# Samples' queries and one mixing step moved among the value tiles, softmax steps of the samples set one to two pages apart, two sizes of a split table changed

## The chip, the cores and the metric

One Trainium2 chip, one of its cores. The time is that of one execution on the device, in microseconds (us). The kernel before takes 904.75 us (median of 3 runs, 904.45 to 905.07). Engines are named as in the profile: PE (matrix products), PEld (its weight loads), DVE (vector), ACT (scalar functions), POOL (general) and SP (issues most DMAs).

## The reference

One layer of a decoder for 512 prompt rows and 8 sample rows (one new token each, 4096 cached positions in 32 pages of 128). Cut to what the change touches:

```python
z = rmsnorm(x) @ w_in
u, v = gelu(z[OFF_U:OFF_V]), gelu(z[OFF_V:])          # 512 columns each
q = rope(rmsnorm(...))                                # 8 heads, 64 + 32
sg = u * (einsum('gts,bcsgd->bctgd', tril(w_s), v) + b_s)   # mixing in chunks of 128 rows
# a sample b attends to its 4096 cached rows c and itself:
k_n = rmsnorm(einsum('bkr,rhd->bkhd', c, w_uk)) * k_norm_w
p = softmax((q_nope @ k_n + q_rope @ k_rope) * SCALE)
attn = (p @ c) @ w_uv
h = x + concat(attn, sg) @ w_o
h = h + conv_ffn(rmsnorm(h)); ...
```

## The kernel before

A product in full float32 precision is made of three products of a high and a low part (`mm3`, L148 to L151), so nearly all PE work carries the lines L149, L150 and L151. `split` (L135) makes the parts: ACT casts the high one (L138 or L140), DVE or POOL subtracts (L133, L146). The scheduler of the tile framework sets the order on each engine from the program's order, the readiness that it estimates and the hints `issue_after` (not before that instruction) and `keep_in_program_order`; engines work through their order strictly, and the same order runs every time.

**Value tiles.** The rows are five tiles: 0 to 3 of 128 prompt rows, 4 of the 8 samples. `v_mm(t)` makes v of a tile with 24 products of 128x512 and ACT takes its gelu out of PSUM (`v_out`, L520). `mix(t)` then multiplies v, split into `sq` tiles, with the masked table `wsr`, whose mask is applied on DVE (L883) and which is split into `wsh` (ACT) and `wsl` (DVE, L133). The program's order is `v_mm(4)`, the table, `v_mm(0)`, `mix(4)`, `v_mm(1)`, `mix(0)`, `v_mm(2)`, `mix(1)`, `v_mm(3)`, then the load of the function table with exp and ln (`preload_act_table_set`, L898), `mix(2)`, `mix(3)`; the prompt's first head is transposed in between (`t_step`, L645).

**Samples' queries.** In front of all that stand, for the 8 samples: eight transposes of the queries (L484), their scaling into `qgT` (L485), the score of the own key `snall` (L486 to L494), the product of queries and `w_ukT` (L500) into `qtil` (L502), and `qbd`, the rotary part (L506).

**Pages.** `s_page` handles one cached page of one sample: six products (`mm3` twice) into one of three PSUM tiles `mm`, ACT squares them (L761) and copies out the scores (`raw`, L762), DVE sums the squares (`ss`, L763) out of one of three `sq` tiles. A page's PSUM tile is free when `raw` has been copied. There are 32 pages to a sample and 256 in all: two in each of the prompt's 16 attention blocks, the rest, for samples 1 to 7, one behind the other. The softmax of sample b is spread over the pages of sample b+1 by a table of steps, page number to work (`steps`, L812 ff.): variance and ln, exp and square, the factor on `raw`, the correction (`newton`), the addition to the scores, maxima, their transpose (L794), `mx_all` (L797, L798), their broadcast by PE (`mx_b`, L801), subtraction, exp, sum, and the product with the values (L838). For the last sample it runs beside the first products with `w_o` (`o_half`). SGS names the groups of four pages behind which a part of the mixed rows `sgr` is split for those products.

Of the kernel before, what the change touches and what calls it, by code (L numbers as in the profile page):

```python
# [39 lines left out]
NG = 10  # L40
NAT = 8
KRQ = 4
SGS = (51, 54, 59, 62)
EF = 3
PF = 2

# [2 lines left out]
def trunk_step(ctx: ExitStack, tc: tile.TileContext, I, O):  # L49
# [429 lines left out]

    qs_, ks_ = qtok[4], ktok[4]  # L480
    qgT = const([96, 8, 8], F32, "qgT")
    ps = ms()
    for h in range(8):
        nc.tensor.transpose(ps[:96, h * 8:h * 8 + 8], qs_[:8, h * DQ:(h + 1) * DQ], ident[:8, :8])  # L484
    nc.vector.tensor_scalar(qgT.rearrange("p h b -> p (h b)"), ps[:96, 0:64], gq96[:, 0:1], None, op0=ALU.mult)  # L485
    nc.vector.tensor_mul(h96(ks_, 8)[:, :, 0:DN], h96(ks_, 8)[:, :, 0:DN], gqk8[:, 0:1].to_broadcast([8, 8, DN]))  # L486
    nc.vector.tensor_mul(qs_[:8, 0:768], qs_[:8, 0:768], ks_[:8, 0:768])
    snew = S()
    nc.vector.tensor_reduce(snew[:8, 0:8], h96(qs_, 8), axis=AX.X, op=ALU.add)
    nc.vector.tensor_scalar(snew[:8, 0:8], snew[:8, 0:8], SCALE, None, op0=ALU.mult)  # L490
    snall = const([128, 8, 8], F32, "snall")
    nc.gpsimd.memset(snall, NEG)
    nc.vector.tensor_mul(snall[:8], eye8[:, 0].rearrange("p (b h) -> p b h", b=8), snew[:8, 0:8].unsqueeze(1).to_broadcast([8, 8, 8]))
    nc.vector.tensor_add(snall[:8], snall[:8], eye8[:, 1].rearrange("p (b h) -> p b h", b=8))  # L494

    wukT = WR()
    nc.sync.dma_start(wukT[0:64, 0:1024], I["w_ukT"])
    ps = ms()
    for h in range(8):
        nc.tensor.matmul(ps[:, h * 8:h * 8 + 8], wukT[0:64, h * 128:(h + 1) * 128], qgT[0:64, h], start=True, stop=True)  # L500
    qtil = const([128, 8, 8], F32, "qtil")
    nc.vector.tensor_copy(qtil.rearrange("p h b -> p (h b)"), ps[:, 0:64])  # L502
    qbd = const([128, 8, 4, 8], F32, "qbd")
    nc.gpsimd.memset(qbd, 0.0)
    for j in range(4):
        nc.scalar.copy(qbd[32 * j:32 * j + 32, :, j, :], qgT[64:96].rearrange("p h b -> p b h"))  # L506


    bsb = G()
# [12 lines left out]
    def v_mm(t):  # L522
        t0, n = TOK[t]
        sl = slice(t0, t0 + n)
        ps = mm()[:n, 0]
        for j in range(4):
            wh, wl = wget(k_v[j], 3 - j)
            for i in range(2):
                mm3(ps, xh[j][:, i, sl], xl[j][:, i, sl], u3(wh, 2, 512)[:, i], u3(wl, 2, 512)[:, i],
                    j == 0 and i == 0, j == 3 and i == 1)  # L530
        v_out(t, ps)

    def mix(t):
        t0, n = TOK[t]
        v = vg[t]
        if t == 3:
            nc.sync.dma_start(O["vp"], v[:, 0:512])
        if t == 4:
            nc.sync.dma_start(O["vs"], v[:8, 0:512])
            mx = G()  # L540
            m3 = mx[:8, 0:512].rearrange("p (g d) -> p g d", g=8)
            nc.vector.tensor_mul(m3, v[:8, 0:512].rearrange("p (g d) -> p g d", g=8), ws8[:, 0].unsqueeze(2).to_broadcast([8, 8, 64]))
            nc.vector.tensor_add(m3, m3, ws8[:, 1].unsqueeze(2).to_broadcast([8, 8, 64]))
            ps = ms()
            for gp in range(4):
                nc.tensor.transpose(ps[:, gp * 8:gp * 8 + 8], mx[:8, gp * 128:(gp + 1) * 128], ident[:8, :8])
# [75 lines left out]

    pq_ = {}

    def prep_items(hp):

        qk = [None] * 4
        pq_[hp] = [None, qk]
# [11 lines left out]
        def t_step(c, w):  # L640
            h = 2 * hp + c
            src, sc = ((qtok, gq96), (ktok, None))[w]
            ps = ms()
            for t in range(4):
                nc.tensor.transpose(ps[:96, t * 128:(t + 1) * 128], src[t][:, h * DQ:(h + 1) * DQ], ident)  # L645
# [124 lines left out]
    def s_softmax(b):  # L770
# [24 lines left out]

        def mx_all():
            nc.vector.tensor_reduce(m2[:8, 0:1], hold["t"][:8, 0:128], axis=AX.X, op=ALU.max)  # L797
            nc.vector.tensor_scalar(m2[:8, 8:16], ident[:8, 0:8], m2[:8, 0:1], None, op0=ALU.mult)  # L798

        def mx_b():  # L800
            after_keys(lambda: nc.tensor.matmul(hold["t"][:, 128:136], ones[:8], m2[:8, 8:16], start=True, stop=True))  # L801
# [2 lines left out]
            nc.gpsimd.tensor_scalar(ss, ss, 1.0 / DN, EPS, op0=ALU.mult, op1=ALU.add)  # L804
            act(y0, ss, AF.Ln)

        def rstd():
            act(y0, y0, AF.Exp, scale=-0.5)
            act(t, y0, AF.Square)

        with_qbd[16] = mx_t
        steps.update({  # L812
            4: var,
            5: rstd,
            6: lambda: nc.vector.tensor_mul(raw, raw, y0),
            7: lambda: newton(raw, ss, raw, t),
            8: lambda: nc.vector.tensor_add(sc[:, 0:256], sc[:, 0:256], raw),
            9: lambda: nc.vector.tensor_reduce(m1[:, 0:8], s3.rearrange("p c h -> p h c"), axis=AX.X, op=ALU.max),
            17: mx_all,
            20: mx_b,  # L820
            21: lambda: nc.vector.tensor_sub(s3, s3, hold["t"][:, 128:136].unsqueeze(1).to_broadcast([128, 33, 8])),
            23: lambda: act(sc, sc, AF.Exp),
            24: lambda: nc.vector.tensor_reduce(psum[:, 0:8], s3.rearrange("p c h -> p h c"), axis=AX.X, op=ALU.add),
            27: lambda: s_pv(b),
            29: lambda: s_out(b),
        })
# [81 lines left out]
    blocks = [(hp, qb) for hp in range(4) for qb in range(4)]  # L908
    pa_score(0, 0)
# [360 lines left out]
```

## Time and profile before

| what | value |
|---|---|
| median of 3 runs | 904.75 us |
| the profiled execution's own time | 907.9 us |
| its span, first to last instruction | 906.0 us |
| granted PE clock, mean | 0.989 of full |
| DVE, ACT, POOL busy | 645.2, 503.6, 215.0 us (71%, 56%, 24%) |
| table loads on ACT (ACT_TABLE_LOAD) | 9, of 1.28 us each |
| value tiles 0 to 3 | from 81.9 to 117.4 us |
| pages of samples 1 to 7 alone | from about 204 to 408 us |

Busy time of an engine is the time in which one of its instructions runs; a product on PE overlaps the next one. The granted clock is the share of full speed that PE was given in a stretch.

### The profile page before, as it was taken

The page shows a single profiled execution, that of the slowest core. Times are in us where ns is not written, and L with a number is a line of the kernel's source. Part 1 is how long each engine was busy: PE and PEld are TensorE (multiplying, and loading weights), DVE is VectorE, ACT ScalarE, POOL GpSimd, SP SyncE. Part 2 cuts the span into 40 slices and gives each one's busy share as a digit, 9 for nine tenths or more (in the row PEclk, how much of TensorE's full clock was granted, in tenths as well). Part 3 has the DMA queues.
Part 4 walks back from the last instruction along what each step waited for, and adds up shares of the span by engine and source line. Part 5 has one row for each costly group of instructions (what it writes and reads, how often), then busy time and mean ns, then how long its engine had stood idle before and what let it go on. Part 6 is the DMA issues. An engine that isn't in the chain of part 4 may idle for free.

```text
span 906.0 us, 20621 instructions
## 1 busy us (share of the span) xinstructions
PE 884.8 (98%) x7847; PEld 843.4 (93%) x7847; DVE 645.2 (71%) x1093; ACT 503.6 (56%) x1182; POOL 215.0 (24%) x243
## 2 busy tenths in 40 slices
PE   8998999999999999999999999999999999999997
PEld 6896878889999999889999999999999999999997
DVE  6579676668888898796669776337775437766774
ACT  6573368778888888784446443124443224455561
POOL 4004851237777777730000000000000000000000
PEclk9999999999999999999999999999999999999999
DMA  6332160243667664613332222322222322323311
GB/s 220 99 97 82 48 186 1 80 137 98 180 186 214 190 194 135 203 59 110 84 122 88 89 88 75 113 94 94 94 93 71 116 94 83 97 84 100 117 59 60
DMA packets 65347, 100.43 MB, mean 111 GB/s; under 512 B 13841, under 2 KB 47770, under 8 KB 65250
## 3 DMA queue, kind: packets, MB, share of 16 engines
q1 hardware_dynamic: 63202, 94.93, 33.2%
q0 software_dynamic: 2048, 4.20, 1.8%
q8 instruction: 62, 1.02, 0.5%
q14 instruction: 35, 0.29, 0.1%
HBM read 95.95 MB, written 3.15 MB: 109 GB/s over the span
## 4 chain that ended last, share of the span: by engine, by line
PE 77%; DVE 7%; ACT 6%; issue 4%; DMA 3%; SPq 3%; POOL 1%; ACTq 0%; POOLq 0%; DVEq 0%
PE mm L149 23%; PE mm L150 23%; PE mm L151 23%; DVE ss L763 2%; SPq L605 2%; PE ms L838 1%; ACT sq L761 1%; ACT wr L670 1%; PE ms L697 1%; PE ms L149 1%; DMA wr<-w_u 1%; PE ms L151 1%; PE ms L150 1%; DVE wr L673 1%; PE ms L156 1%
## 5 line engine op out<-in xcount | busy, mean ns | idle before, releaser
L149 PE MATMUL mm<-u,w 128*128 128x260 f32 x1392 | 395.2, 284 | 0.1
L151 PE MATMUL mm<-u,w 128*128 128x260 f32 x1392 | 394.7, 284 | 0.0
L150 PE MATMUL mm<-u,w 128*128 128x260 f32 x1392 | 394.1, 283 | 0.0
L150 PEld LDWEIGHTS mm<-u,w 128*128 128x128 f32 x1392 | 263.0, 189 | 0.2
L151 PEld LDWEIGHTS mm<-u,w 128*128 128x128 f32 x1392 | 262.8, 189 | 0.2 <-issue 0.2
L149 PEld LDWEIGHTS mm<-u,w 128*128 128x128 f32 x1392 | 262.5, 189 | 0.5 <-PE mm L151 0.2
L133 DVE TENSOR_TENSOR w<-wr,w 128x1024 fp32r<-128x1024 f32 (+1 forms) x94 | 112.6, 1199 | 106.1 <-issue 54.0
L763 DVE TENSOR_REDUCE ss<-sq 128x8 f32<-128x512 f32 x256 | 166.8, 678 | 26.4 <-ACT sq L761 21.9
L138 ACT CAST w<-wr 128x1024 fp32r<-128x1024 f32 (+1 forms) x94 | 96.5, 1031 | 140.4 <-PE mm L151 127.1
L761 ACT ACTIVATE sq<-mm 128x512 f32<-128x512 f32 x256 | 153.1, 610 | 33.2 <-PE mm L151 18.7
L149 PE MATMUL mm<-wuk,a 128*128 128x260 f32 x416 | 123.4, 297 | 2.5 <-ACT raw L762 2.1
L151 PE MATMUL mm<-wuk,a 128*128 128x260 f32 x416 | 118.4, 285 | 0.0
L150 PE MATMUL mm<-wuk,a 128*128 128x260 f32 x416 | 118.3, 284 | 0.0
L149 PEld LDWEIGHTS mm<-wuk,a 128*128 128x128 f32 x416 | 79.1, 190 | 8.2 <-ACT raw L762 6.3
L150 PEld LDWEIGHTS mm<-wuk,a 128*128 128x128 f32 x416 | 79.1, 190 | 0.0
L151 PEld LDWEIGHTS mm<-wuk,a 128*128 128x128 f32 x416 | 79.0, 190 | 0.0
L592 POOL DMA_INDIRECT wr<-krT,idx x64 | 62.4, 974 | 14.1 <-issue 6.4
L1082 ACT ACTIVATE a<-abuf,cst 128x512 f32<-128x512 f32 x44 | 35.9, 816 | 39.9 <-DVE abuf L1080 38.8
L1083 DVE SCALAR_TENSOR_TENSOR a<-abuf,cst,a 128x512 f32<-128x512 f32 x44 | 33.0, 751 | 25.7 <-ACT a L1082 25.4
L133 POOL TENSOR_TENSOR a<-u,a 128x512 fp32r<-128x512 f32 x34 | 44.2, 1301 | 17.0 <-ACT a L719 15.0
L762 ACT COPY raw<-mm 128x8 f32<-128x8 f32 x256 | 44.5, 174 | 0.0
L138 ACT CAST u<-a 128x520 fp32r<-128x520 f32 x24 | 15.1, 627 | 43.7 <-DVE a L1121 43.3
(307 smaller groups left out, 1324.4 us busy)
## 6 DMA issues: line engine op xcount, KB each, us to landing
wr<-w_ffi SPq DMA_DIRECT2D x44, 512.0 KB
u<-pages SPq DMA_DIRECT2D x152, 128.0 KB
w<-pages SPq DMA_DIRECT2D x104, 128.0 KB
wr<-w_ffo SPq DMA_DIRECT2D x16, 512.0 KB
wr<-w_o SPq DMA_DIRECT2D x8, 512.0 KB
wr<-w_pg SPq DMA_DIRECT2D x8, 512.0 KB
wr<-w_ffo SPq DMA_DIRECT2D x8, 384.0 KB
a<-xT SPq DMA_DIRECT2D x8, 260.0 KB
```

Of the source, the lines that this page charges most:

```text
L133: return (nc.vector if eng == "v" else nc.gpsimd).tensor_sub(dl, src, dh.bitcast(F32))
L138: nc.scalar.copy(dh, src)
L149: nc.tensor.matmul(out, lh, rh, start=start, stop=False)
L150: nc.tensor.matmul(out, lh, rl, start=False, stop=False)
L151: return nc.tensor.matmul(out, ll, rh, start=False, stop=stop)
L592: nc.gpsimd.indirect_dma_start(krT[:, g * 128:(g + 1) * 128], None, I["krT"], bass.IndirectOffsetOnAxis(ap=idx.bitcast(U32)[:, b * 8 + g:b ...
L605: page_dma.append(nc.sync.dma_start(pv[:, j], I["pages"][bass.ds(rs[j], 1)].rearrange("a p f -> (a p) f")))
L761: squares.append(nc.scalar.activation(u3(sq, 2, 256), ps[:, :, 0:256], AF.Square))
L762: nc.scalar.copy(raw[:, c * 8:c * 8 + 8].rearrange("p (a h) -> p a h", a=2), ps[:, :, 256:260])
L763: nc.vector.tensor_reduce(ss[:, c * 8:c * 8 + 8], sq.rearrange("p (h d) -> p h d", d=DN), axis=AX.X, op=ALU.add)
L1082: nc.scalar.activation(c[:, 0:T], a[:, 2:T + 2], AF.Identity, scale=cw[:, m, 2:3], bias=cw[:, m, 3:4])
L1083: nc.vector.scalar_tensor_tensor(c[:, 0:T], a[:, 1:T + 1], cw[:, m, 1:2], c[:, 0:T], op0=ALU.mult, op1=ALU.add)
```

## The change

Four edits:

1. The samples' queries become `s_queries(after)` (transposes, `qgT`, `qbd`, `snall`), called behind `v_mm(1)` with its last product as `after`; the product with `w_ukT` becomes `s_folded`, behind `v_mm(2)`. `mix(4)` moves behind `v_mm(1)`. The memsets of `snall` and `qbd` stay in front.
2. `mix(2)` moves in front of the load of the function table. The first head's transposes all come behind `v_mm(3)`.
3. Softmax steps: 4, 5, 6, 7, 8, 9 become 3, 4, 5, 6, 7, 9, 10, 12: exp and square are two steps, `newton` is two steps. `mx_all` 17 to 18, `mx_b` 20 to 21, subtraction 21 to 22, exp 23 to 24, sum 24 to 25. In `mx_all` the product of the unit matrix and the maximum is a `tensor_mul` with a broadcast operand in place of a `tensor_scalar`.
4. SGS becomes (59, 60, 62, 63) from (51, 54, 59, 62).

```diff
-SGS = (51, 54, 59, 62)
+SGS = (59, 60, 62, 63)
...
-    ps = ms()
-    for h in range(8):
-        nc.tensor.transpose(ps[:96, h * 8:h * 8 + 8], qs_[:8, h * DQ:(h + 1) * DQ], ident[:8, :8])
-    nc.vector.tensor_scalar(qgT.rearrange("p h b -> p (h b)"), ps[:96, 0:64], gq96[:, 0:1], None, op0=ALU.mult)
...
+    def s_queries(after):
+
+        ps = ms()
+        with tc.issue_after(after.ins):
+            for h in range(8):
+                nc.tensor.transpose(ps[:96, h * 8:h * 8 + 8], qs_[:8, h * DQ:(h + 1) * DQ], ident[:8, :8])
+        nc.vector.tensor_scalar(qgT.rearrange("p h b -> p (h b)"), ps[:96, 0:64], gq96[:, 0:1], None, op0=ALU.mult)
...
+    def s_folded(after):
+        ps = ms()
+        with tc.issue_after(after.ins):
+            for h in range(8):
+                nc.tensor.matmul(ps[:, h * 8:h * 8 + 8], wukT[0:64, h * 128:(h + 1) * 128], qgT[0:64, h], start=True, stop=True)
+        nc.vector.tensor_copy(qtil.rearrange("p h b -> p (h b)"), ps[:, 0:64])
...
-            nc.vector.tensor_scalar(m2[:8, 8:16], ident[:8, 0:8], m2[:8, 0:1], None, op0=ALU.mult)
+            nc.vector.tensor_mul(m2[:8, 8:16], ident[:8, 0:8], m2[:8, 0:1].to_broadcast([8, 8]))
...
-            4: var,
-            5: rstd,
+            3: var,
+            4: lambda: act(y0, y0, AF.Exp, scale=-0.5),
+            5: lambda: act(t, y0, AF.Square),
             6: lambda: nc.vector.tensor_mul(raw, raw, y0),
-            7: lambda: newton(raw, ss, raw, t),
...
     v_mm(0)
-    mix(4)
-    p0 = prep_items(0)
-    p0 = prep_items(0)
-    v_mm(1)
+    v1 = v_mm(1)
+    s_queries(v1)
+    mix(4, v1)
     mix(0)
-    p0[0]()
-    v_mm(2)
+    v2 = v_mm(2)
+    s_folded(v2)
     mix(1)
-    p0[1]()
-    p0[2]()
-    v_mm(3)
+    v3 = v_mm(3)
+    mix(2)
     tc.keep_in_program_order(nc.scalar.preload_act_table_set("natural_log_exp_and_others"))
     wuv = G()
...
-    mix(2)
+    p0 = prep_items(0, v3)
+    for f in p0[:4]:
+        f()
     mix(3)
-    p0[3]()
     p0[4]()
```

Behind line 480 the changed kernel's line numbers are higher by 7 to 12: L898 is L906 there, the gelu L520 is L527, the softmax's functions L781 are L793, the exp of the prompt L670 is L682.

The order on ACT behind value tile 2, before (the rows end with the prompt's first exp, L670; `g` is a gelu's result or the high part of a head, `sq` the high part of a value tile, `a` and `g` from `ms` the first head's parts):

```order
L520 ACTIVATE g_1306<-mm_1281,rtok 128x512
L898 ACT_TABLE_LOAD
L138 CAST sq_1467<-g_1306 128x512
L138 CAST a_1498<-ms_1493 96x512
L637 COPY g_1507<-ms_1502 128x512
L670 ACTIVATE wr_1521,s_1519<-mm_1509,s_1518 128x128 x2
```

and of the change:

```order
L138 CAST sq_1281<-g_1216 128x512
L906 ACT_TABLE_LOAD
L527 ACT_TABLE_LOAD
L527 ACTIVATE g_1279<-mm_1254,rtok 128x512
L140 ACTIVATE g_1444<-ms_1439,gq_385 96x512
L138 CAST sq_1476<-g_1279 128x512
L138 CAST g_1453<-ms_1448 96x512
L140 ACTIVATE a_1462<-ms_1457,gq_385 96x512
L138 CAST a_1471<-ms_1466 96x512
L646 COPY g_1507<-ms_1502 128x512
L682 ACT_TABLE_LOAD
L682 ACTIVATE wr_1521,s_1519<-mm_1509,s_1518 128x128 x2
```

The load that the program asks for now stands ahead of value tile 3's gelu; a load for the gelu stands behind it, and one for exp ahead of the prompt's first exp. In all there are 29 table loads on ACT, 9 before: these two more, two at each of the eight softmaxes, and two at the norm ahead of the feed-forward part.

The order on ACT in the softmax of sample 0, among the pages of sample 1 (L761 and L773 the square of a page, L762 and L774 its scores), before:

```order
L762 COPY raw_2634<-mm_2718 128x8
L781 ACTIVATE g_2613<-ss_1553 128x256
L761 ACTIVATE sq_2738<-mm_2731 128x512
L762 COPY raw_2634<-mm_2731 128x8
L781 ACTIVATE g_2613<-g_2613 128x256
L761 ACTIVATE sq_2751<-mm_2744 128x512
```

and of the change:

```order
L774 COPY raw_2634<-mm_2689 128x8
L793 ACT_TABLE_LOAD
L793 ACTIVATE g_2613<-ss_1553 128x256
L773 ACTIVATE sq_2727<-mm_2720 128x512
L774 COPY raw_2634<-mm_2720 128x8
L793 ACT_TABLE_LOAD
L793 ACTIVATE g_2613<-g_2613 128x256
L773 ACTIVATE sq_2739<-mm_2732 128x512
```

A table load now stands ahead of the ln and another, one page later, ahead of the exp; before there was none at either.

The order on DVE behind the key tiles of the prompt, which makes the table for `mix(0)` (`w` the masked table, `wr` its low part, `u` and `g` queries and keys), of the change:

```order
L473 TENSOR_TENSOR u_653<-u_653,g_577 128x8x32
L893 TENSOR_TENSOR w_1070<-w_1070,cst 128x1024
L373 TENSOR_TENSOR g_857<-u_653,g_573 128x256
L374 TENSOR_TENSOR g_857<-u_653,g_573 128x8x16
L375 TENSOR_TENSOR g_857<-u_653,g_573 128x8x16
L499 TENSOR_TENSOR u_580<-u_580,cst 8x8x64
L376 TENSOR_TENSOR u_653<-g_857 128x8x32
L133 TENSOR_TENSOR wr_1074<-w_1070,wr_1073 128x1024
L133 TENSOR_TENSOR sq_1166<-g_1102,sq_1165 128x512
```

Before, L485 stood where L893 stands, and L883 and the split of `wr` came nine and fifteen rows behind it. On PE the eight transposes L495 now stand behind all 48 products of value tiles 0 and 1, and directly behind them the products of `mix(0)`; before they stood (as L484) among the products of value tile 0, and those of `mix(0)` behind tile 1 and beside tile 2.

More of the change, by code (lines that the diff above doesn't have):

```diff
@@ L481, in trunk_step @@
     qgT = const([96, 8, 8], F32, "qgT")
-    ps = ms()
-    for h in range(8):
-        nc.tensor.transpose(ps[:96, h * 8:h * 8 + 8], qs_[:8, h * DQ:(h + 1) * DQ], ident[:8, :8])
-    nc.vector.tensor_scalar(qgT.rearrange("p h b -> p (h b)"), ps[:96, 0:64], gq96[:, 0:1], None, op0=ALU.mult)
[L486 to L489, printed above, removed]
@@ L490, in trunk_step @@
-    nc.vector.tensor_scalar(snew[:8, 0:8], snew[:8, 0:8], SCALE, None, op0=ALU.mult)
     snall = const([128, 8, 8], F32, "snall")
+    qtil = const([128, 8, 8], F32, "qtil")
+    qbd = const([128, 8, 4, 8], F32, "qbd")
     nc.gpsimd.memset(snall, NEG)
-    nc.vector.tensor_mul(snall[:8], eye8[:, 0].rearrange("p (b h) -> p b h", b=8), snew[:8, 0:8].unsqueeze(1).to_broadcast([8, 8, 8]))
-    nc.vector.tensor_add(snall[:8], snall[:8], eye8[:, 1].rearrange("p (b h) -> p b h", b=8))
+    nc.gpsimd.memset(qbd, 0.0)
@@ L528, in v_mm, with mix @@
             for i in range(2):
-                mm3(ps, xh[j][:, i, sl], xl[j][:, i, sl], u3(wh, 2, 512)[:, i], u3(wl, 2, 512)[:, i],
-                    j == 0 and i == 0, j == 3 and i == 1)
+                last = mm3(ps, xh[j][:, i, sl], xl[j][:, i, sl], u3(wh, 2, 512)[:, i], u3(wl, 2, 512)[:, i],
+                           j == 0 and i == 0, j == 3 and i == 1)
         v_out(t, ps)
-    def mix(t):
+        return last
+    def mix(t, after=None):
         t0, n = TOK[t]
@@ L545, in mix @@
             for gp in range(4):
-                nc.tensor.transpose(ps[:, gp * 8:gp * 8 + 8], mx[:8, gp * 128:(gp + 1) * 128], ident[:8, :8])
+                with tc.issue_after(after.ins):
+                    nc.tensor.transpose(ps[:, gp * 8:gp * 8 + 8], mx[:8, gp * 128:(gp + 1) * 128], ident[:8, :8])
             for gp in range(4):
@@ L623, in trunk_step, with prep_items @@
     pq_ = {}
-    def prep_items(hp):
+    def prep_items(hp, after=None):
         qk = [None] * 4
@@ L643, in t_step @@
             ps = ms()
-            for t in range(4):
-                nc.tensor.transpose(ps[:96, t * 128:(t + 1) * 128], src[t][:, h * DQ:(h + 1) * DQ], ident)
+            with ExitStack() as es:
+                if after:
+                    es.enter_context(tc.issue_after(after.ins))
+                for t in range(4):
+                    nc.tensor.transpose(ps[:96, t * 128:(t + 1) * 128], src[t][:, h * DQ:(h + 1) * DQ], ident)
             th, tl = (A(F32R), A(F32R)) if c else (G(F32R), G(F32R))
```

38 lines of the change are left out of this document (19 added, 19 removed).

## The prediction

> **What bounds the kernel now.** I read the page first, then PE's waits, then the granted clock in stretches.
>
> ```profile
> span 906.0 us, 20621 instructions
> PE 884.8 (98%) x7847; PEld 843.4 (93%) x7847; DVE 645.2 (71%) x1093; ACT 503.6 (56%) x1182; POOL 215.0 (24%) x243
> PE mm L149 <- ACT raw L762: 2.9, 10, 0.8
> PE ms L484 <- DVE u L376: 2.6, 1, 2.6
> PE ms L801 <- DVE s L798: 1.9, 1, 1.9
> ```
>
> PE is busy for 884.8 of 906.0 us, so it is the bound, and only 21.2 us of idle time can be won without giving it less work. The change takes no product away. The three waits are those that it aims at: 2.9 us in ten pieces for PSUM tiles of the pages, 2.6 us once for the samples' queries, 1.9 us once for the maxima. Whatever makes PE wait anew is paid in full, and it may be paid twice, as the clock shows in stretches of 3.41 us (the first number is the stretch's length, the second PE's busy time; the third last column is the granted clock):
>
> ```profile
> 84.00:87.41 3.41, 1.15 (x11) 1.04 (x12) 3.41 (x10) 0.00 (x0) 3.41 (x2) 1.00 0.00 0
> 87.41:90.83 3.42, 3.42 (x10) 2.64 (x9) 3.42 (x9) 1.38 (x5) 3.42 (x2) 0.50 0.00 0
> 90.83:94.24 3.41, 3.41 (x23) 2.86 (x23) 3.41 (x5) 0.52 (x1) 3.41 (x5) 1.00 0.03 5
> 94.24:97.65 3.41, 3.41 (x10) 2.66 (x9) 3.41 (x6) 2.36 (x5) 3.41 (x3) 0.50 0.00 0
> 118.13:121.54 3.41, 2.42 (x20) 2.06 (x19) 2.62 (x7) 2.53 (x4) 3.33 (x5) 1.00 0.84 248
> 121.54:124.96 3.42, 3.42 (x47) 3.27 (x49) 2.17 (x6) 0.59 (x1) 1.37 (x5) 1.00 0.80 221
> 363.90:367.32 3.42, 1.56 (x14) 1.33 (x12) 3.42 (x4) 2.22 (x8) 3.24 (x4) 1.00 0.21 58
> 367.32:370.73 3.41, 3.41 (x16) 3.41 (x16) 2.43 (x5) 1.06 (x3) 0.72 (x1) 0.50 0.65 186
> ```
>
> On this grid the clock is 1.00 or 0.50 for a whole stretch. A stretch with 2.26 us idle (84.00) or 1.86 us (363.90) is followed by one at half clock, which costs 3.41 / 2 = 1.7 us; one with 0.99 us idle (118.13) is not. The stretch from 90.83 is full, but more than half of it are the small products L500, and it too is followed by half clock. So idle time above some point between 0.99 and 1.86 us in a stretch costs 1.7 us more.
>
> **The table loads.** The order of the change has 29 loads of ACT's function table, the order before 9. The end of the kernel before shows what ln and exp cost where the common table is not loaded:
>
> ```profile
> 859.76 1.28 ACT L165 ACT_TABLE_LOAD   x1
> 861.05 0.64 ACT L165 ACTIVATE g<-g 128x520 f32<-128x520 f32 x1
> 861.71 1.28 ACT L166 ACT_TABLE_LOAD   x1
> 863.00 0.64 ACT L166 ACTIVATE g<-g 128x520 f32<-128x520 f32 x1
> ```
>
> One load takes 861.05 - 859.76 = 1.29 us of ACT's time, and ln followed by exp needs two. In the change the load that the program asks for runs ahead of value tile 3's gelu, which loads another table; so every softmax of a sample now has two loads, one page apart. The Trainium skill (ScalarE: Activation LUTs, What ACT_TABLE_LOAD costs) has the same 1283 ns, but adds a drain of about 1380 ns to each switch. The rows show no drain: the function behind the load starts 0.01 us after it; by that page each load would cost twice as much.
>
> **Pages.** Seven of the softmaxes run among pages that stand one behind the other. How much ACT can be late there, before:
>
> ```profile
> 348.20 0.28 PE L149 MATMUL mm<-wuk,a 128*128 128x260 f32 x1
> 352.55 0.28 PE L149 MATMUL mm<-wuk,a 128*128 128x260 f32 x1
> 349.12 0.60 ACT L761 ACTIVATE sq<-mm 128x512 f32<-128x512 f32 x1
> 349.62 0.16 ACT L762 COPY raw<-mm 128x8 f32<-128x8 f32 x1
> 352.41 0.62 ACT L761 ACTIVATE sq<-mm 128x512 f32<-128x512 f32 x1
> 352.94 0.47 ACT L781 ACTIVATE g<-g 128x256 f32<-128x256 f32 x1
> 353.25 0.64 ACT L761 ACTIVATE sq<-mm 128x512 f32<-128x512 f32 x1
> 353.73 0.46 ACT L781 ACTIVATE g<-g 128x256 f32<-128x256 f32 x1
> 354.04 0.21 ACT L762 COPY raw<-mm 128x8 f32<-128x8 f32 x1
> 354.31 0.39 PE L149 MATMUL mm<-wuk,a 128*128 128x260 f32 x1 [0.16 <-ACT raw L762]
> ```
>
> The first two rows are the first products of pages six apart: 0.725 us a page. A page begun at S has its square at S + 0.92 and its PSUM tile free at S + 1.58 (348.20 to 349.12 and 349.78); PE needs the tile for the third page behind it at S + 2.18. So ACT may be 0.6 us late. Back to back ACT needs 0.53 us for a page and 0.31 us for an exp or a ln (352.41, 352.94, 353.25), so it catches up 0.19 us with each page.
>
> Now the change, with S the start of page 4. ACT is done with page 3 at S + 0.75; load 1.29 and ln 0.32 put page 4's square to S + 2.36 and its tile's release to S + 3.02; page 7 can begin at S + 3.08 instead of S + 2.18: **0.9 us** of wait. ACT goes on at S + 2.89: load, exp, page 5's square at S + 4.49, released at S + 5.15; PE had finished page 7 at S + 3.80: **1.4 us**. The square of page 6 adds 0.1 us. Together 2.4 us a sample, against the 2.9 us in ten waits, 0.4 us a sample, that the change's wider steps may spare: +2.0 us net, times 7 = **+14.0 us**. From both sides: 2.58 us of loads less the whole lateness that ACT has free (0.6 and two pages' 0.19) gives 1.6 us a sample, 11 us; nothing absorbed gives 2.6 us, 18 us.
>
> The waits of a sample lie within 3.1 us. Wherever the grid cuts them, one stretch holds 1.2 to 2.4 us idle; with the deciding point between 0.99 and 1.86 I take two samples in three: 7 x 0.65 x 1.7 = **+7.7 us**, from 0 to 12 (every sample).
>
> **Last sample and norm.** Two more chains have the loads and products behind them:
>
> ```profile
> 410.32 0.42 ACT L781 ACTIVATE g<-ss 128x256 f32<-128x256 f32 x1 [1.26 <-POOL ss L804]
> 414.28 0.27 PE L794 MATMUL ms<-cst,s 128*8 128x128 f32 x1 [0.48 <-DVE s L818]
> 473.33 0.64 ACT L165 ACTIVATE g<-g 128x520 f32<-128x520 f32 x1 [1.08 <-DVE g L232]
> 476.82 1.31 DVE L1080 TENSOR_TENSOR abuf<-mm,rstd_b 128x520 f32<-128x520 f32 x2
> 477.66 0.36 PE L149 MATMUL mm<-u,w 128*128 128x260 f32 x1
> ```
>
> In the last sample's softmax the first load fits into ACT's idle 1.26 us ahead of the ln; the second delays the chain by 1.29. PE waits for that chain already (0.48 us), and its transpose stands one product earlier: +1.4 us (0.9 to 2.6). In the norm the first load has 1.08 us of idle time, so the chain is 1.5 us later; DVE frees the first PSUM tile at about 477.5, PE takes it at 477.66: +1.3 us (0 to 1.6). Each makes a half-clock stretch possible; I add 0.8 us for either (0 to 1.7). **+4.3 us** in all.
>
> **Value tiles.** The wait of 2.56 us goes: the transposes stand behind 48 products, to which PE comes 11 us later. But `mix(0)` now follows directly, and its table is late.
>
> ```profile
> 83.08 0.39 PE L151 MATMUL mm<-w,u 128*128 128x512 f32 x1
> 83.30 0.40 PE L149 MATMUL mm<-w,u 128*128 128x512 f32 x1
> 93.07 0.41 DVE L376 TENSOR_TENSOR u<-g 128x256 f32<-128x256 f32 x1
> 95.53 1.20 DVE L883 TENSOR_TENSOR w<-w,cst 128x1024 f32<-128x1024 f32 x1
> 99.59 1.21 DVE L133 TENSOR_TENSOR wr<-w,wr 128x1024 fp32r<-128x1024 f32 x1
> ```
>
> Value tile 0 begins at 81.92; 48 products at 0.23 us (83.08 to 83.30) and the transposes end at 93.5. On DVE the mask (1.2 us) moves in front of the rows that ended with L376 at 93.4, L485 leaves them: 94.4; then the table's low part (1.2) 95.6 and tile 0's low part (0.6): PE waits from 93.7 to 96.2, some 2.3 us, in the place of 2.56. Both orders have two half-clock stretches here, behind the wait and behind the small products. The extra loads L906 and L527 stand where ACT waits for value tile 3; L682 runs while DVE takes maxima. On POOL the gathers of the rotary keys move behind the products of `mix(0)` with u, and one behind those of `mix(1)`; PE reads them only behind the prompt's first scores, so I give that nothing, and the +2.0 below is its bound too. SP's queue keeps its order of pages; they wait for tiles that value tile 3 frees at the same time as before. I take **-1.0 us**; from -4.3 (no new wait, its half clock gone with it) to +2.0 (a like wait, and L682's load exposed).
>
> **Maxima and splits.** The 1.9 us wait came from one of eight L798:
>
> ```profile
> 364.62 2.33 DVE L798 TENSOR_SCALAR s<-cst,s 8x8 f32<-8x8 f32 x1
> 365.67 1.25 POOL L133 TENSOR_TENSOR a<-u,a 128x512 fp32r<-128x512 f32 x1
> ```
>
> It ended when this subtraction on POOL ended (366.95 and 366.92), so it stood behind POOL. The `tensor_mul` that takes its place is another form; if that doesn't stand behind POOL, the wait and its half clock go, 1.9 + 1.7 = **-3.6 us**, and I take that (0 if the stall comes again). The Trainium skill (SBUF — State Buffer, Who interferes with whom) speaks against it: a VectorE operation with two SBUF inputs also contends with a GpSimd instruction that reads SBUF. By that page the stall could come again, and the sum would be 3.6 us higher; no row here has this form at this place. The four splits of SGS keep their cost and stand in the last sample's pages: 0 (0 to +1, one more cast of 0.5 us near another).
>
> **Sum**: 14.0 + 7.7 + 4.3 - 1.0 - 3.6 = +21.4 us on the profiled 907.9, and so on the median: 904.75 + 21.4, about **926 us**. The profiled execution is 3.2 us above the median; if the stall of L798 is part of that, the sum on the median is up to 3.6 higher.
>
> **Rivals.** *ACT's idle time takes the loads* (not slower): in this row, PE, PEld, DVE and ACT busy among the lone pages,
>
> ```profile
> 204.00:408.00 204.00, 198.85 (x2418) 188.04 (x2416) 181.43 (x308) 169.94 (x541) 145.60 (x156) 0.99 0.54 163
> ```
>
> ACT is idle for 34 us, the loads are 14 x 1.29 = 18. It decides if PE can be further ahead than 0.6 us at those pages; then the waits of 2.9, the maxima's 3.6 and the value tiles' 1.0 us are won: 897 us. Against it: three functions of 0.31 us already made PE wait (354.31). Chance 0.05.
>
> *No half clock*, if waits in two pieces do not count together: 926 - 7.7 - 1.6 = 917 us; 0.17. *Every sample brings it*, half of them two stretches: 10.5 x 1.7 = 17.9 in the place of 7.7, 936 us; 0.13. *A load costs twice*, as a drain would: 16 exposed loads at 1.29 more: about 947 us; 0.03. *The two-operand form is blocked like the old one*: 930 us; 0.15. *The change does not do what it says*, the value tiles' wait going without another: 926 - 3.3 = 922 us if the table is ready when PE comes, 0.07. The forecast itself, 926: 0.40.
>
> The range 910 to 940 leaves out the first, the load at twice its cost, and the tails of the two clock cases (some 0.08). A measurement here tells 0.2% (1.8 us) from no change: faster 0.05, same 0.01, slower 0.94.
>
> **What would show it.** Twenty-nine table loads of 1.28 us; PE waiting for `raw` about 2.4 us behind each pair of loads; the mean clock of the pages below 0.99; PE waiting about 2 us ahead of `mix(0)` near 94 us; L806 waiting about 2 us near 415. The forecast is wrong if those waits for `raw` are under 1 us a sample, or if a stretch at half clock follows none of them.

## The result and the profile after

The changed kernel takes 935.57 us (median of three executions, 934.26 to 937.2), the kernel before, beside it, 904.91 us (904.45 to 905.85): a ratio of 1.034, 95% interval 1.032 to 1.036. A fourth execution of the changed kernel took 2891.8 us; it has no profile, its cause is not known, and it is not counted. The profiled execution's own time is 934.26 us, against 907.9 before: +26.4.

The page's lines on the span and the engines, changed kernel:

```profile
span 932.0 us, 20634 instructions
PE 890.2 (96%) x7847; PEld 848.5 (91%) x7847; DVE 645.1 (69%) x1093; ACT 530.9 (57%) x1202; POOL 214.4 (23%) x243
```

The work is the same, product for product (x7847). PE's busy time grew by 5.4 us, though it has no more to do; the other 20.6 us of the longer span are idle time. ACT has 20 instructions and 27.3 us more. PE's waits (line, what released it; us in sum, how often, the longest):

```profile
PE mm L149 <- ACT raw L774: 17.9, 15, 1.3
PE ms L806 <- DVE s L828: 4.1, 4, 1.9
PE mm L149 <- DVE abuf L1089: 2.6, 1, 2.6
PE mm L149 <- ACT sq L138: 2.3, 1, 2.3
PE ms L555 <- DVE g L551: 2.1, 1, 2.1
PE mm L694 <- DVE wr L685: 1.2, 2, 1.0
```

The 2.9 us in ten pieces for `raw` became 17.9 us in fifteen, about two pieces a sample. The waits of 2.6 us (L484) and 1.9 us (the maxima) are gone. Of the others, `abuf` and L555 are new; the waits at L806, for `sq` and at L694 were 0.5, 0.9 and 0.2 us before. One pair of waits in the timeline, ACT and PE of the changed kernel (start, length; in brackets the idle time before it and its releaser; a copy at 273.98, between the second row and the third, is not shown):

```profile
272.97 0.62 ACT L731 CAST a<-w 128x512 fp32r<-128x512 f32 x1
273.49 0.59 ACT L773 ACTIVATE sq<-mm 128x512 f32<-128x512 f32 x1
274.16 1.28 ACT L793 ACT_TABLE_LOAD   x1
275.45 0.42 ACT L793 ACTIVATE g<-ss 128x256 f32<-128x256 f32 x1
275.77 0.58 ACT L773 ACTIVATE sq<-mm 128x512 f32<-128x512 f32 x1
276.25 0.16 ACT L774 COPY raw<-mm 128x8 f32<-128x8 f32 x1
276.43 1.28 ACT L793 ACT_TABLE_LOAD   x1
277.72 0.42 ACT L793 ACTIVATE g<-g 128x256 f32<-128x256 f32 x1
278.04 0.58 ACT L773 ACTIVATE sq<-mm 128x512 f32<-128x512 f32 x1
278.52 0.16 ACT L774 COPY raw<-mm 128x8 f32<-128x8 f32 x1
276.46 0.39 PE L149 MATMUL mm<-wuk,a 128*128 128x260 f32 x1 [1.28 <-ACT raw L774]
278.73 0.46 PE L149 MATMUL mm<-wuk,a 128*128 128x260 f32 x1 [1.28 <-ACT raw L774]
```

ACT does in turn a load, a function of the softmax and one page; each time PE stands 1.28 us, as long as the load, until the copy `raw` has freed a PSUM tile. The function starts 0.01 us after its load, so again no drain shows. The first row matters too: ACT casts the high part of coming pages (L731, 0.62 us) one page ahead of the first load, in six of the seven samples, and in these both waits are 1.27 to 1.29 us. In the first sample the cast is two pages ahead, and the first wait is 1.09 us. The clock on the 3.41 us grid of this execution (the first number behind the stretch is its length, the second PE's busy time, the third last the granted clock):

```profile
275.49:278.90 3.41, 1.16 (x7) 0.95 (x8) 1.42 (x2) 3.38 (x9) 2.05 (x3) 1.00 0.77 224
278.90:282.32 3.42, 3.42 (x17) 3.42 (x18) 3.42 (x7) 2.49 (x9) 1.44 (x2) 0.50 0.73 238
306.21:309.62 3.41, 1.67 (x12) 1.25 (x10) 1.01 (x2) 3.37 (x6) 2.00 (x3) 1.00 0.76 214
309.62:313.04 3.42, 2.59 (x12) 2.59 (x13) 3.15 (x5) 2.84 (x10) 2.35 (x3) 0.50 0.78 224
313.04:316.45 3.41, 3.41 (x17) 3.41 (x17) 3.06 (x6) 1.92 (x6) 0.00 (x0) 0.50 0.69 215
401.78:405.20 3.42, 2.14 (x18) 1.93 (x17) 1.52 (x3) 3.37 (x8) 3.26 (x4) 1.00 0.19 62
405.20:408.61 3.41, 2.12 (x16) 1.84 (x16) 2.31 (x5) 3.40 (x10) 3.18 (x4) 1.00 0.57 178
```

Where both waits fall into one stretch (275.49, 2.25 us idle) half clock follows. Where the grid parts them (401.78 and 405.20, 1.28 and 1.29 us idle) it does not. Five stretches of the pages are at half clock (278.90, 309.62, 313.04, 343.76, 374.48), one before.

By stages of the two profiled executions, with borders at the first product of value tile 0, at the first and last start of the pages' rotary products (L156, `qbd`) and at the last product with the values: up to value tile 0 81.9 and 79.6 us, -2.3; the value tiles 42.9 to 45.2 us, **+2.3**; the pages 268.2 to 289.4, **+21.2**; the last sample's softmax 26.8 to 28.8, **+2.0**; the rest, with the norm, **+2.8**. That is the +26.0 us of the span. The earlier start can't be put down to the change: the execution before has a half-clock stretch at 8.9 us that this one has not, and the profile of e1 below, which has the change's program there, has one at 8.1 us.

The pages' part is 15.7 us more idle time of PE and 5.5 us more busy time. In the idle time, within these borders, the waits for `raw` grew from 2.5 to 17.9 us, L806 waits 1.5 us and L694 1.0 us more, and the 1.9 us of the maxima are gone: 16.0 us. The busy time is that of four more half-clock stretches, at most 1.7 us each.

### The profile page after: what moved, and what is told of

It reads as the page before. It is cut to its first block, busy times and chain, and to the rows that moved or that the text cites. A ratio compares the mean times of both kernels' runs of the same rounds, so it can differ in the third digit from the quotient of the medians.

```text
span 932.0 us, 20634 instructions
## 1 busy us (share of the span) xinstructions
PE 890.2 (96%) x7847; PEld 848.5 (91%) x7847; DVE 645.1 (69%) x1093; ACT 530.9 (57%) x1202; POOL 214.4 (23%) x243
## 4 chain that ended last, share of the span: by engine, by line
PE 76%; ACT 9%; DVE 7%; issue 3%; DMA 2%; POOL 2%; SPq 1%; ACTq 0%; DVEq 0%; POOLq 0%
PE mm L149 23%; PE mm L151 22%; PE mm L150 22%; DVE ss L775 2%; ACT L793 2%; PE ms L848 1%; ACT wr L682 1%; ACT sq L773 1%; PE ms L709 1%; PE ms L149 1%; DVE w L133 1%; ACT g L793 1%; PE ms L151 1%; PE ms L150 1%; DVE wr L685 1%
## 5 line engine op out<-in xcount | busy, mean ns | idle before, releaser
L773 ACT ACTIVATE sq<-mm 128x512 f32<-128x512 f32 x256 | 151.3, 604 | 33.4 <-PE mm L151 20.1
L149 PE MATMUL mm<-wuk,a 128*128 128x260 f32 x416 | 125.6, 302 | 15.7 <-ACT raw L774 15.6
L151 PE MATMUL mm<-wuk,a 128*128 128x260 f32 x416 | 120.8, 290 | 0.0
L150 PE MATMUL mm<-wuk,a 128*128 128x260 f32 x416 | 120.8, 290 | 0.0
L149 PEld LDWEIGHTS mm<-wuk,a 128*128 128x128 f32 x416 | 81.7, 196 | 20.8 <-ACT raw L774 18.7
L150 PEld LDWEIGHTS mm<-wuk,a 128*128 128x128 f32 x416 | 81.9, 197 | 0.0
L151 PEld LDWEIGHTS mm<-wuk,a 128*128 128x128 f32 x416 | 81.7, 196 | 0.0
L774 ACT COPY raw<-mm 128x8 f32<-128x8 f32 x256 | 43.6, 170 | 0.0
```

The source lines that it names most:

```text
L149: nc.tensor.matmul(out, lh, rh, start=start, stop=False)
L150: nc.tensor.matmul(out, lh, rl, start=False, stop=False)
L151: return nc.tensor.matmul(out, ll, rh, start=False, stop=stop)
L773: squares.append(nc.scalar.activation(u3(sq, 2, 256), ps[:, :, 0:256], AF.Square))
L774: nc.scalar.copy(raw[:, c * 8:c * 8 + 8].rearrange("p (a h) -> p a h", a=2), ps[:, :, 256:260])
```

## The experiments

The theory: the whole loss comes from 20 table loads, and these come from one line's place. With `mix(2)` in front of the asked-for load, this load runs ahead of value tile 3's gelu, which throws the common table out again; from there on ln and exp fetch two tables in turn. Rivals: the other edits cost a good part of it; half clock does not hang on how the waits are grouped. In the table "raw" and "L806" are PE's waits in us (the last by its line in the changed kernel; L794 in the others), "half" the half-clock stretches of the pages, "pages" the time from the first to the last rotary product, all from the profiled execution. Ratios are against the kernel before on the same chip (medians 904.7, 905.7 and 905.3 us).

| kernel | loads | raw | L806 | half | pages | median us | ratio (95%) |
|---|---|---|---|---|---|---|---|
| before | 9 | 2.9 | 0.5 | 1 | 268.2 | 904.9 | 1 |
| changed | 29 | 17.9 | 4.1 | 5 | 289.4 | 935.6 | 1.034 (1.032 to 1.036) |
| e1_load_first | 9 | 1.5 | 4.8 | 0 | 266.7 | 907.3 | 1.002 (1.001 to 1.003) |
| e2_load_last | 9 | 1.5 | 4.8 | 0 | 266.7 | 905.1 | 1.001 (0.999 to 1.003) |
| e3_mix2_alone | 29 | 17.3 | 1.8 | 8 | 293.5 | 938.5 | 1.036 (1.030 to 1.041) |
| e4_loads_apart | 29 | 10.9 | 13.3 | 4 | 297.0 | 943.2 | 1.043 (1.040 to 1.046) |
| e5_loads_three_pages | 29 | 15.2 | 7.9 | 2 | 288.7 | 930.0 | 1.026 (1.024 to 1.028) |
| e6_early_maximum | 9 | 2.6 | 0.7 | 0 | 262.8 | 898.7 | 0.992 (0.990 to 0.994) |
| e7_old_maxima_form | 9 | 1.5 | 4.7 | 0 | 266.9 | 902.8 | 0.997 (0.995 to 0.998) |
| e8_mix4_later | 9 | 2.6 | 0.7 | 0 | 263.9 | 898.1 | 0.992 (0.989 to 0.995) |
| e9_form_alone | 9 | 1.9 | 0.6 | 0 | 266.1 | 905.1 | 1.000 (0.998 to 1.001) |
| e10_steps_alone | 9 | 1.3 | 0.6 | 0 | 261.8 | 899.7 | 0.993 (0.991 to 0.994) |
| e11_loads_in_four | 20 | 11.5 | 3.4 | 5 | 285.1 | 924.2 | 1.020 (1.018 to 1.022) |
| e12_steps_and_form | 9 | 1.3 | 0.7 | 0 | 261.9 | 901.0 | 0.994 (0.992 to 0.996) |

**Is it the loads?** Two ways to take them out of the changed kernel, and one edit of the change alone. `pre` stands for the line with `preload_act_table_set`.

```diff
 # e1_load_first, against the changed kernel
-    mix(2)
     pre
+    mix(2)
 # e2_load_last, against the changed kernel
     mix(2)
-    pre
...
     mix(3)
+    pre
     p0[4]()
 # e3_mix2_alone, against the kernel before
     v_mm(3)
+    mix(2)
     pre
...
-    mix(2)
     mix(3)
```

> The changed kernel with one line put back: the table's load that the program asks for stands in front of mix(2) again, so that it comes behind value tile 3's gelu; all other edits of the change stay. The ScalarE stream then has 9 table loads in the place of 29. Theory (the loads are the cost): waits of PE for raw fall from 17.9 us to about 3, the half-clock stretches of the pages go, the norm's wait goes, 898 to 907 us. Rival (the other edits cost half or more of the 31 us: the softmax steps, the queries behind value tile 1, the later small groups): 918 us or more.

> The changed kernel with mix(2) left where the change puts it, and the asked-for load moved back instead, behind mix(3), where ScalarE runs it with its own instructions of that place: 9 loads. Theory: the order of mix(2) itself costs nothing, only the loads do: 898 to 907 us, within 3 us of the run with the load in front of mix(2). Rival (the new order of mix(2) costs by itself, on VectorE or in the value tiles): 5 us or more above that run.

> The kernel before with one edit of the change alone: mix(2) in front of the asked-for load. The ScalarE stream then has 29 loads. Theory: 20 loads are the whole cost, 928 to 938 us, waits for raw of 15 us or more and four or more stretches at half clock more than before. Rival (it takes the other edits too, such as the softmax steps on pages 3 and 4, to make the loads hurt): under 918 us.

All three came out as the theory has it, e1 and e3 some 0.3 and 0.5 us above their ranges. With 9 loads the changed kernel is within 0.3% of the kernel before (907.3 and 905.1 us), with the load ahead of `mix(2)` or behind `mix(3)`; e1's 2.2 us above e2 lie within the intervals, and its profile has a wait of 2.4 us in the value tiles that e2 has not. The one edit alone brings 29 loads to the kernel before and 938.5 us, as much as the whole change. So the loads are the loss, and the other edits together are worth about nothing. The waits of e2:

```profile
PE ms L806 <- DVE s L828: 4.8, 7, 0.7
PE ms L555 <- DVE g L551: 2.1, 1, 2.1
PE mm L149 <- ACT raw L774: 1.5, 2, 1.0
```

The pieces at L806 are a new wait, hidden in the changed kernel's sum: PE comes for the transposes of the maxima before VectorE has the maximum, which the change put on page 12 in the place of 9.

**What does a load cost, and when does the clock fall?** Exponential and logarithm further apart, with all loads left in, and loads in four samples only.

```diff
 # e4_loads_apart, against the changed kernel; the steps behind them move to 9, 10, 11, 13, 14, 15
-            4: lambda: act(y0, y0, AF.Exp, scale=-0.5),
+            8: lambda: act(y0, y0, AF.Exp, scale=-0.5),
 # e5_loads_three_pages; the steps behind them move to 7, 8, 9, 10, 11, 12
-            4: lambda: act(y0, y0, AF.Exp, scale=-0.5),
+            6: lambda: act(y0, y0, AF.Exp, scale=-0.5),
 # e11_loads_in_four, in var()
+            if b == 4:
+                pre
             act(y0, ss, AF.Ln)
```

> The changed kernel with all its loads, but the softmax's second function (the exponential) five pages behind the logarithm in the place of one; what follows it moves back by 4 pages as far as the maximum. Theory (a load makes ScalarE late, PE waits what is beyond its lead, and a stretch gets half clock only where more than about 1 us of waiting falls in it): twice as many separate waits of about 1 us, in sum 12 to 18 us, but at most two stretches at half clock in the pages in the place of 5: 925 to 933 us. Rival (half clock comes by chance or with every wait): as many stretches as the changed kernel or more, 935 us or more. Rival (the lead takes up a single load): waits for raw under 6 us in sum, 915 us or less.

The time went the other way, to 943.2 us: the expectation failed, and the time is where the first rival had it. But the waits are not those that were to be tested. The waits for `raw` fell to 10.9 us; VectorE became late instead:

```profile
PE ms L806 <- DVE s L828: 11.2, 6, 2.1
PE mm L149 <- ACT raw L774: 10.9, 9, 2.1
PE mm L149 <- issue: 4.7, 6, 0.9
```

The edit had put the maximum on page 15, one page ahead of its transposes, and each such wait of 2 us is in one piece. (A seventh, of 2.1 us, the profile puts down to `ss`, so L806 waits 13.3 us in all; "issue" is waiting for nothing that it shows.) In the grid of this run, as in the table before:

```profile
322.68:326.09 3.41, 1.34 (x12) 1.14 (x11) 3.41 (x6) 1.08 (x5) 1.87 (x2) 1.00 0.40 127
326.09:329.50 3.41, 3.41 (x17) 3.18 (x16) 2.38 (x6) 2.33 (x8) 2.05 (x2) 0.50 0.00 0
390.94:394.36 3.42, 1.62 (x14) 1.62 (x15) 3.31 (x7) 1.09 (x5) 1.32 (x2) 1.00 0.73 200
394.36:397.77 3.41, 3.41 (x28) 3.25 (x28) 2.98 (x7) 2.89 (x10) 2.47 (x3) 1.00 0.01 5
```

The stretch with the wait at L806 (2.07 us idle) is followed by half clock, the one with 1.80 us idle is not. All four half-clock stretches of these pages follow 1.9 us or more of one wait, three times at L806, once for `raw`; none follows a lone wait of 1.3 us for `raw`. The run mixed two things and was repeated with a shorter distance:

> The changed kernel with all 29 loads, the exponential three pages behind the logarithm in the place of one, and the steps behind it pulled together, so that the maximum stays on page 12. It repeats the run with five pages, where the maximum stood one page ahead of its transposes and PE waited 11.2 us for VectorE at L806. If that run was slow by this crowding: L806 waits 5 us or less in sum, and the time 926 to 936 us, not above the changed kernel. If separated loads are dear by themselves (ScalarE gets its lead back between them only in part, so each of two waits is paid in full): waits of PE in the pages of 24 us or more in sum, and 938 us or more.

930.0 us, below the changed kernel and inside the expectation, though L806 waits more than it allows (7.9 us). The waits in sum are no smaller than in the changed kernel (15.2 + 7.9 against 17.9 + 4.1 us): a load three pages from the next is still paid. In the pages alone PE is idle for 26.3 us here and for 23.0 us in the changed kernel, so the waits of 24 us or more that the second case of the expectation named are there; its time, 938 us or more, is not. What went is half clock: in all the pages with samples alone (204 us on) one stretch is left, behind the one stretch with 2.04 us idle, a single wait of that length, and those with a single wait of about 1 us keep their clock. One of each:

```profile
285.63:289.05 3.42, 2.35 (x49) 2.10 (x49) 3.42 (x7) 2.01 (x7) 3.10 (x4) 1.00 0.79 222
289.05:292.46 3.41, 3.41 (x31) 3.41 (x30) 3.12 (x7) 2.97 (x9) 1.30 (x2) 1.00 0.77 227
401.68:405.10 3.42, 1.38 (x12) 1.17 (x11) 1.04 (x2) 2.92 (x9) 3.26 (x4) 1.00 0.10 16
405.10:408.51 3.41, 3.41 (x17) 3.25 (x16) 2.33 (x5) 3.38 (x10) 3.17 (x4) 0.50 0.49 168
```

In the two profiled executions these add up to little: the pages have 4.0 us less busy time and 3.3 us more idle time, 288.7 against 289.4 us. The mean granted clock is 0.990 to 0.991 in all four executions of this run and 0.980 to 0.983 in the three of the changed kernel, so the higher clock is not of the one profile alone.

> The changed kernel with the common table asked for once more ahead of the logarithm of the fifth sample: the pages of the first four samples keep two loads each, the other four and the first norm behind them have none. Theory (each sample with loads costs by itself, some 2.3 us of waits and, in every second one, 1.7 us of half clock; the norm 2.6): against the run with 9 loads 4 x 2.3 + 2 to 3 x 1.7 us and 1 us in the value tiles: 916 to 923 us. Rival (the loads hurt only where the samples' and the prompt's work meet, or only at the end and in the norm): under 912 us, or over 928 us.

924.2 us, 1 us above the expectation. Four samples with loads lengthen the pages by 285.1 - 266.7 = 18.4 us against e2, 4.6 us a sample; the changed kernel's seven by 289.4 - 266.7 = 22.7 us, 3.2 us a sample. The waits behind a sample's two loads are about the same: 10.6 us over four samples here, 17.7 us over seven there, so 2.5 to 2.7 us each. The load that is asked for once more costs a wait of 1.3 us in the fifth sample. Most of the rest is the clock: five half-clock stretches for four samples here, five for seven there. So a sample's loads cost some 2.6 us of waits, and between none and two times 1.7 us of clock, by where the grid cuts them.

**What do the other edits give?** First the steps and the value tiles without loads, from e2 on.

```diff
 # e6_early_maximum, against e2_load_last
-            7: lambda: nc.vector.scalar_tensor_tensor(t, ss, -0.5, t, op0=ALU.mult, op1=ALU.mult),
-            9: lambda: nc.vector.scalar_tensor_tensor(raw, t, 1.5, raw, op0=ALU.add, op1=ALU.mult),
-            10: lambda: nc.vector.tensor_add(sc[:, 0:256], sc[:, 0:256], raw),
-            12: lambda: nc.vector.tensor_reduce(m1[:, 0:8], s3.rearrange("p c h -> p h c"), axis=AX.X, op=ALU.max),
+            7: lambda: newton(raw, ss, raw, t),
+            8: lambda: nc.vector.tensor_add(sc[:, 0:256], sc[:, 0:256], raw),
+            9: lambda: nc.vector.tensor_reduce(m1[:, 0:8], s3.rearrange("p c h -> p h c"), axis=AX.X, op=ALU.max),
 # e8_mix4_later, against e6_early_maximum
-    mix(4, v1)
     mix(0)
     v2 = v_mm(2)
+    mix(4, v2)
```

> The run with the asked-for load behind mix(3), and in it the softmax's VectorE steps pulled together again: both products of the Newton step on page 7, the sum on 8, the maximum on 9 in the place of 12; the ScalarE steps stay on 3, 4 and 5. Theory (the later maximum gives back what the maxima's new form wins): the 7 waits at L806 for the maximum, 4.8 us in sum, go to under 1 us, and the time is 3 to 5 us below that run: 900 to 902 us. Rival (those waits are not on the path that sets the end, or return as waits for raw): within 1.5 us of it.

> The run with the early maximum, and in it mix(4) behind the third value tile in the place of the second, its transposes behind that tile too. Theory (the wait of 2.1 us at L555, inside the third tile, is what took the place of the old wait in front of the transposes of the samples' queries, and brings a half-clock stretch): that wait goes, 2 to 4 us below the run with the early maximum: 897 to 900 us. Rival (another wait in the value tiles takes its place): within 1 us of that run.

e6 does better than both kernels: 898.7 us, 0.8% below before, and 1.3 us below its expectation. Its pages are 3.9 us shorter than e2's, as the waits show:

```profile
PE mm L149 <- ACT raw L774: 2.6, 3, 1.1
PE ms L555 <- DVE g L551: 2.1, 1, 2.1
...
PE ms L806 <- DVE s L827: 0.7, 1, 0.7
```

In e8 the wait at L555 is gone from the list, and the pages begin 2.8 us earlier (119.0 against 121.8), but the median is 0.7 us lower with four runs from 895.7 to 900.5: by time the two can't be told apart. The expected 2 to 4 us did not show: a wait of 1.2 us at L657 has come, and a half-clock stretch is left in its value tiles too.

Then the maxima's product and the steps by themselves; the form is the one of the diff of the change.

```diff
 # e7_old_maxima_form, against e2_load_last
-            nc.vector.tensor_mul(m2[:8, 8:16], ident[:8, 0:8], m2[:8, 0:1].to_broadcast([8, 8]))
+            nc.vector.tensor_scalar(m2[:8, 8:16], ident[:8, 0:8], m2[:8, 0:1], None, op0=ALU.mult)
 # e9_form_alone: the reverse, against the kernel before
 # e10_steps_alone, against the kernel before; the steps behind the maximum one page later
-            4: var,
-            5: rstd,
+            3: var,
+            4: lambda: act(y0, y0, AF.Exp, scale=-0.5),
+            5: lambda: act(t, y0, AF.Square),
...
-            17: mx_all,
-            20: mx_b,
+            18: mx_all,
+            21: mx_b,
 # e12_steps_and_form: both of these
```

> The run with the asked-for load behind mix(3), with the maxima's product in its old form (the scalar of the operand in the place of the broadcast one). Theory as forecast (the old form holds VectorE up once, 1.9 us, and brings a stretch at half clock): one wait of about 2 us at L813 comes back, 2 to 4 us above that run: 907 to 909 us. Rival (the stall hung on one meeting with GpSimd and does not come at the new steps): within 1 us of it, and no wait there over 0.5 us.

> The kernel before with one edit of the change alone: the maxima's product in its new form (the broadcast operand), at the old steps. Theory as forecast (the new form ends the wait of 1.9 us at L801 and the half-clock stretch behind it): 901 to 903 us, no wait at L801 over 0.5 us. Rival (the stall comes from what else VectorE and GpSimd do at that page; after the run with the old form at the new steps, which had no stall, this is the likelier): the wait stays at about 2 us, within 1.5 us of the kernel before.

> The kernel before with the softmax steps alone: logarithm, exponential and square on pages 3, 4 and 5, what follows the maximum one page later, the maximum on page 9 as before, the old form of the maxima's product. Theory (the steps, not the form, take the maxima's stall away): no wait at L801 over 0.5 us, no half clock in the pages, waits for raw about 1 us less, 900 to 902 us. Rival (the form is what counts): the wait at L801 stays, 904 to 906 us.

> The kernel before with both of these edits, steps and form, and none of the others: the samples' queries, mix(4), mix(2) and the late small groups stay as before. It is the run with the early maximum without these. Theory (most of what that run wins, 0.8%, comes from the pages; the new place of the queries changes one wait of 2.6 us for one of 2.1 us and saves one half-clock stretch): 899 to 902 us, 1 to 3 us above that run. Rival (the win comes from the queries' new place): 903 us or more.

The form does nothing for the time: with it alone (e9) the kernel is where it was. What counts is when the product runs. With the old form at the new steps (e7) no product of the eight is slow; with the new form at the old steps (e9) one is. The summary of the product's line in e7 and in e10 (ns: shortest, median, longest; first and last start), and the timeline of e9 at the slow one:

```profile
L810 DVE TENSOR_SCALAR s<-cst,s x8: 207/208/220, 220.5 to 411.1; 8x8 f32<-8x8 f32 x8
L798 DVE TENSOR_SCALAR s<-cst,s x8: 209/210/614, 222.6 to 406.8; 8x8 f32<-8x8 f32 x8
```

```profile
362.70 1.31 POOL L133 TENSOR_TENSOR u<-u,u 128x520 fp32r<-128x520 f32 x1
362.89 2.35 DVE L798 TENSOR_TENSOR s<-cst,s 8x8 f32<-8x8 f32 x1
363.96 1.26 POOL L133 TENSOR_TENSOR a<-u,a 128x512 fp32r<-128x512 f32 x1
```

It begins 0.2 us into one subtraction of POOL and ends with the next (365.24 and 365.22), as the old form did. The Trainium skill (SBUF — State Buffer, Who interferes with whom) has a VectorE operation with two SBUF inputs contend with a GpSimd instruction that reads SBUF; this row agrees, with 2.35 us in the place of 0.14. The 14 profiles of this case have 112 of these products. Five are slow, three of the old form (2.33 us before, 3.17 in e3, 0.61 in e10) and two of the new one (2.35 in e9, 0.62 in e12). They are the only ones that have a subtraction of POOL beside them for more than 0.1 us, and each ends within 0.05 us of the end of one. So the steps help by letting the product miss POOL's subtractions, or meet only the end of one (e10, e12). That moving POOL's work would free it was not tried. e9's time is that of the kernel before: the wait of 1.9 us is there, though no half clock followed it this time.

e7's time was expected 2 to 4 us above e2's, or by the rival within 1 us. It is 0.35% below the kernel before (0.997), e2 is not (1.001), and their intervals do not touch. The profiles have the same pages (266.9 and 266.7 us) and nearly the same spans (901.1 and 901.7 us), and the two ran on different chips, so where these 0.4% come from stays open.

The steps alone (e10) win 0.75%; e12, with the form added, and e6, with the queries, `mix(2)`, `mix(4)` and the later groups added as well, have intervals that overlap with e10's and with each other's. So what of the change is of use is its table of steps, with the maximum left where it was. e10 itself is 0.3 us below its range, e12 inside. The later groups (SGS) have had no run of their own.

## Why the prediction was right, and where not

*Bound and table loads*: right. PE is the bound, 29 loads of 1.28 us, no drain, and what PE waits for is paid in full.

*Pages, +14.0*: right, +15.4 by PE's waits for `raw`. The walk gave 0.9 + 1.4 us to a pair, the rows have 1.28 + 1.28, the bound at which nothing is absorbed. The walk had ACT done with page 3 at S + 0.75 and so 0.6 us of lead; it left out the cast L731, which took 0.55 us of that lead before the load began (page 4 begins at 272.84, the load at 274.16). Not seen either was that the change's wider steps, which were to spare 0.4 us a sample, do so (raw 1.5 us in e2), but put the maximum so late that L806 waits: 4.2 us in e2 in seven samples, 2.2 in the changed kernel, where PE itself is late.

*Half clock, +7.7*: right. Five new stretches, at most 8.5 us, in four of seven samples, one with two. The rows at 275.49 and 401.78 and e5's clock show that the grouping of the waits decides; how many stretches a kernel gets is chance of the grid (5 in the changed kernel, 8 in e3), and so is part of the agreement.

*Last sample and norm, +4.3*: +2.0 and +2.8 us. The norm's term was mis-sized: PE waits 2.6 us there (predicted 1.3, at most 1.6), and a half-clock stretch follows at 504. The first load was to run in ACT's idle time ahead of the function. It did not; it began only when the function's operand was there, behind the same idle time as before:

```profile
496.56 1.28 ACT L165 ACT_TABLE_LOAD   x1 [1.06 <-DVE g L232]
```

So both loads stand on the norm's chain. In the last sample the first load did run ahead (430.82, before `ss` was ready at 432.04), and the wait at L806 is 1.9 us where it was 0.5, the 1.4 us of the forecast; no half clock.

*Value tiles, -1.0*: wrong, +2.3 from value tile 0's first product on, where the forecast went to +2.0. That the first page begins at 124.8 us in both executions is luck of the earlier start. "PE waits from 93.7 to 96.2" ahead of `mix(0)` did not happen: the table's low part was ready at 91.6, 4 us earlier than the walk had it (2.3 of these are the earlier start), and PE waited 0.2 us. The row of the changed kernel's timeline:

```profile
90.40 1.21 DVE L133 TENSOR_TENSOR wr<-w,wr 128x1024 fp32r<-128x1024 f32 x1
```

In the place of this wait stand 2.1 us at L555 (the transposes of `mix(4)` inside value tile 2) and 2.3 us ahead of `mix(3)`, where 0.9 us were before. L682's load, which was counted as hidden, makes PE wait 1.0 us at L694, in the first pages.

*Maxima, -3.6*: the wait went, but not for the reason given, so this term came right by luck. "If that doesn't stand behind POOL" failed: the new form stands behind POOL as the old one did (e9), and the steps' new pages took it away (e7, e10). The rival that the two-operand form is blocked was right of the mechanism and wrong of the time.

The sum of +21.4 us stands against +26.4 in the profiled executions and 30.7 between the medians; the executions are 3 us above one median and 1 us below the other. By stages the forecast was 18.1 us for the pages with the maxima (measured 21.2), 2.2 for the last sample (2.0), 2.1 for the norm (2.8) and -1.0 for the value tiles (2.3, with 2.3 less ahead of them).

## What to carry to other kernels

When a step is moved across a load of a function table that the program asks for, count the loads in the order that results: one operation of another table behind it undoes it for everything that follows, and the loss is paid far away, wherever ACT has little lead. When that lead is worked out, count all that ACT does ahead of the load: one cast of 0.62 us took nearly all of it here. Ask how the waits that a change adds are grouped: two short ones in one stretch of the clock's grid cost the clock, the same two in two stretches do not; but setting the loads apart brought other waits (e4, e5). And test the parts of a change alone: a change that lost 3% held one edit that wins 0.75%.

## What the runs showed of the hardware

In a stretch at full clock, half clock follows between 1.5 and 1.9 us of idle PE, where the kernel before left 0.99 to 1.86 open. From 40 us on, in the 14 profiles, each stretch at full clock with 1.85 us idle or more was followed by one at half clock. With 1.49 us or less none was, save three with no idle time at all, of which the one at 90.83 is in the prediction. Between them the idle time alone does not decide: in e10 1.52 us (114.75) lost the clock, in e4 1.80 us (390.94) kept it. In e3:

```profile
245.58:248.99 3.41, 1.84 (x15) 1.84 (x16) 2.64 (x6) 3.34 (x12) 1.06 (x2) 1.00 0.66 190
248.99:252.41 3.42, 3.42 (x34) 3.28 (x36) 3.42 (x7) 3.09 (x10) 2.08 (x2) 1.00 0.72 219
272.89:276.30 3.41, 1.76 (x13) 1.35 (x11) 0.97 (x2) 3.37 (x6) 3.17 (x4) 1.00 0.83 239
276.30:279.72 3.42, 2.36 (x11) 2.36 (x12) 3.16 (x7) 2.77 (x10) 0.71 (x1) 0.50 0.79 219
279.72:283.13 3.41, 3.41 (x17) 3.41 (x17) 2.50 (x5) 1.99 (x7) 0.98 (x1) 0.50 0.68 202
```

1.57 us idle kept the clock, 1.65 us lost it. A stretch that is already at half clock is followed by another with less: 1.06 us idle (276.30 here) and 0.83 us (309.62 in the changed kernel) gave a second one, and so did the smallest such case, 0.51 us (84.01 in e12); 0.48 us (214.86 in e3) did not.
